# Batch norm with ReLU: loading the second half of x in one 8 MB transfer of 64 KB runs

## The chip, the cores and the metric

One core of a Trainium2 chip. The metric is the device time of one execution in microseconds (us), median of several runs. A profile's span is about 1.9 us shorter than the time of the same run (81.9 against 83.77 us). Timed comparisons are of runs at a granted clock of 1.0.

## The reference

```python
# x: (32, 128, 32, 32) float32; gamma, beta, running_mean, running_var: (128,)
normalized = (x - running_mean[None, :, None, None]) / np.sqrt(running_var[None, :, None, None] + eps)
scaled = normalized * gamma[None, :, None, None] + beta[None, :, None, None]
return np.maximum(scaled, 0).astype(np.float32)
```

16.78 MB come in, 16.78 MB go out, and each element needs one multiply, one add and one maximum.

## The kernel before

The 4096 rows (batch x channel) of 4 KB are laid out as 2 halves x 128 partitions x 16 rows, so that one partition of one half is a contiguous run of 64 KB. The whole input fits on the core at once, so every load can be issued at the start. Loads are issued from SyncE, stores from ScalarE. Both queues are served by the same 16 DMA engines: the packet times of loads and stores, divided by 16, add up to 96.2% of the span (prediction).

```python
J = 16
PIECES = (((0, 2), (2, 4), (4, 8), (8, 16)), ((0, 8), (8, 16)))
STORE_CUTS = {(0, 1)}
# ...
    tiles = []
    for t in range(T):
        for a, b in PIECES[t]:
            xt = data.tile([P, b - a, HW], F32, name=f"x{t}_{a}")
            nc.sync.dma_start(out=xt, in_=xr[t, :, a:b, :])
            tiles.append((t, a, b, xt))
# ... scale_t and bias_t are worked out from four small loads ...
    with tc.manual_schedule(engines={mybir.EngineType.Activation}):
        for t, a, b, xt in tiles:
            first = a
            for j in range(a, b):
                nc.scalar.activation(
                    out=xt[:, j - a, :], in_=xt[:, j - a, :], func=ACTF.Relu,
                    bias=bias_t[:, j : j + 1], scale=scale_t[:, j : j + 1],
                )
                if j + 1 == b or (t, j + 1) in STORE_CUTS:
                    nc.scalar.dma_start(
                        out=outr[t, :, first : j + 1, :], in_=xt[:, first - a : j + 1 - a, :]
                    )
                    first = j + 1
```

A piece of n rows is a transfer whose runs are n x 4 KB. One run of one partition is one packet on a DMA engine: the packet records of this kernel have 384 load packets of 32 KB for its three loads of 4 MB. That is 128 packets per transfer, 8 on each of the 16 engines.

## Time and profile before

| | before |
|---|---|
| time, 3 runs | 83.78 us (83.75 to 83.79) |
| span of the profile | 81.9 us |
| start of the first packet of x to end of the last packet | 1.84 to 80.61 us |
| mean time of the packets of one DMA engine | 78.75 us |
| ScalarE busy | 38.5 us, 47% |

### The profile page before, as it was taken

To read this page: it belongs to the slowest core of one execution; us is meant where nothing else is said; L and a number is where in the kernel's file an instruction comes from. 1 tells how busy PE (TensorE), PEld (TensorE's weight loads), DVE (VectorE), ACT (ScalarE), POOL (GpSimd) and SP (SyncE) were. 2 spreads that over 40 slices of the span, in tenths; PEclk is the share of its full clock that TensorE was granted. 3 is DMA by queue.
4 is the path that set the end of the run, shared out by engine and by line. 5 is a ranking of instruction groups with operands and counts; after the bars stand their busy time and mean duration, and the time that the engine had idled before them with its cause. 6 is when DMAs were issued, how large, how long until landed. Compare 5 with 4: busy or idle time off the path is not lost.

```text
span 81.9 us, 119 instructions
## 1 busy us (share of the span) xinstructions
PE 0.7 (1%) x2; PEld 0.5 (1%) x2; DVE 0.8 (1%) x5; ACT 38.5 (47%) x34; POOL 0.8 (1%) x6
## 2 busy tenths in 40 slices
PE   0002000000000000000000000000000000000000
PEld 0002000000000000000000000000000000000000
DVE  0000300000000000000000000000000000000000
ACT  0600377799039999199994199993000000000000
POOL 3000000000000000000000000000000000000000
DMA  2899999989899999979789798996999899799690
GB/s 32 328 425 472 408 448 448 512 352 494 370 448 416 446 418 396 500 296 600 320 380 580 304 464 384 512 512 288 480 512 400 368 512 448 320 512 496 272 512 0
DMA packets 1936, 33.56 MB, mean 410 GB/s; under 512 B 272, under 2 KB 272, under 8 KB 528
## 3 DMA queue, kind: packets, MB, share of 16 engines
q1 hardware_dynamic: 864, 16.78, 48.4%
q10 hardware_dynamic: 1072, 16.78, 47.8%
HBM read 16.78 MB, written 16.78 MB: 410 GB/s over the span
## 4 chain that ended last, share of the span: by engine, by line
DMA 56%; ACT 11%; SPq 0%; issue 0%
DMA x<-in_x_dram 56%; ACT x L96 11%; SPq L52 0%
## 5 line engine op out<-in xcount | busy, mean ns | idle before, releaser
L96 ACT ACTIVATE x<-x,bias_t,scale_t 128x1024 f32<-128x1024 f32 x32 | 37.0, 1228 | 10.3 <-DMA x<-in_x_dram 7.9
L82 ACT ACT_TABLE_LOAD x1 | 1.3, 1283 | 2.6 <-issue 2.6
L82 ACT ACTIVATE std_t<-cols,eps_t 128x16 f32<-128x16 f32 x1 | 0.3, 273 | 4.5 <-PE cols L74 4.5
L74 PE MATMUL cols<-raw,rep 8*128 8x64 f32 x2 | 0.7, 428 | 7.7 <-DMA raw<-in_beta_dram 7.7
L74 PEld LDWEIGHTS cols<-raw,rep 8*128 8x128 f32 x2 | 0.5, 304 | 7.7 <-issue 7.7
L64 POOL TENSOR_SCALAR_AFFINE_SELECT rep<-rep 8x128 f32<-8x128 f32 x1 | 0.4, 392 | 0.1
L84 DVE RECIPROCAL rstd_t<-std_t 128x16 f32<-128x16 f32 x1 | 0.3, 254 | 7.8 <-ACT std_t L82 7.8
L63 POOL MEMSET rep<- 8x128 f32 x1 | 0.2, 195 | 0.3 <-POOLq L124 0.3
L86 DVE TENSOR_TENSOR scale_t<-cols,rstd_t 128x16 f32<-128x16 f32 x1 | 0.2, 175 | 0.1
L90 DVE TENSOR_TENSOR bias_t<-cols,ms_t 128x16 f32<-128x16 f32 x1 | 0.2, 175 | 0.0
L88 DVE TENSOR_TENSOR ms_t<-cols,scale_t 128x16 f32<-128x16 f32 x1 | 0.2, 175 | 0.0
L124 POOL MEMSET const-bfloat16-1.0<- 128x1 bf16 x1 | 0.1, 106 | 0.0
L124 POOL MEMSET const-uint8-127<- 128x1 uint8 x1 | 0.1, 106 | 0.0
L124 POOL MEMSET const-float32-0.0<- 128x1 f32 x1 | 0.1, 103 | 0.3 <-issue 0.3
L124 POOL MEMSET const-float32-1.0<- 128x1 f32 x1 | 0.1, 103 | 0.0
L61 DVE MEMSET eps_t<- 128x1 f32 x1 | 0.1, 59 | 0.9 <-PEq L124 0.9
## 6 DMA issues: line engine op xcount, KB each, us to landing
x<-in_x_dram SPq DMA_DIRECT2D x3, 4096.0 KB, 38.8
out_dram<-x ACTq DMA_DIRECT2D x3, 4096.0 KB, 27.9
x<-in_x_dram SPq DMA_DIRECT2D x2, 1024.0 KB, 5.7
x<-in_x_dram SPq DMA_DIRECT2D x1, 2048.0 KB, 11.2
out_dram<-x ACTq DMA_DIRECT2D x1, 2048.0 KB
out_dram<-x ACTq DMA_DIRECT2D x2, 512.0 KB, 18.8
out_dram<-x ACTq DMA_DIRECT2D x1, 1024.0 KB
raw<-in_running_var_dram ACTq DMA_DIRECT2D x1, 0.5 KB
```

What stands on the lines that cost most here:

```text
L61: nc.vector.memset(eps_t, float(eps))
L63: nc.gpsimd.memset(rep, 1.0)
L64: nc.gpsimd.affine_select(out=rep, in_=rep, compare_op=mybir.AluOpType.is_equal, fill=0.0, base=0, pattern=[[0, P // Q], [-1, Q]], channel ...
L74: nc.tensor.matmul(cols.rearrange("p k j -> p (k j)"), rep.rearrange("q r s -> q (r s)"), raw.rearrange("q k j -> q (k j)"), start=True, s ...
L82: nc.scalar.activation(out=std_t, in_=cols[:, 0, :], func=ACTF.Sqrt, bias=eps_t[:, 0:1], scale=1.0)
L84: nc.vector.reciprocal(out=rstd_t, in_=std_t)
L86: nc.vector.tensor_mul(out=scale_t, in0=cols[:, 1, :], in1=rstd_t)
L88: nc.vector.tensor_mul(out=ms_t, in0=cols[:, 2, :], in1=scale_t)
L90: nc.vector.tensor_sub(out=bias_t, in0=cols[:, 3, :], in1=ms_t)
L96: nc.scalar.activation(out=xt[:, j - a, :], in_=xt[:, j - a, :], func=ACTF.Relu, bias=bias_t[:, j : j + 1], scale=scale_t[:, j : j + 1],)
L124: nc = _bacc.Bacc("TRN2", target_bir_lowering=False, num_devices=1)
```

## The change

The intent: one load instruction and one wait fewer, longer runs, and 16 transfers in all. The semaphores of the transfers rotate through eight, and SyncE waits for them at the end in a fixed order; with 16 transfers the last store's semaphore is the last in it.

```diff
-PIECES = (((0, 2), (2, 4), (4, 8), (8, 16)), ((0, 8), (8, 16)))
+PIECES = (((0, 2), (2, 4), (4, 8), (8, 16)), ((0, 16),))
 
-STORE_CUTS = {(0, 1)}
+STORE_CUTS = {(0, 1), (1, 8)}
```

## The prediction

> **What bounds the kernel now.** I read the page from its second part on: first which row is full from one end to the other, then what the queues carried, and only then the chain.
>
> The slices, the queues and the memory traffic of the page:
>
> ```profile
> ACT  0600377799039999199994199993000000000000
> ...
> DMA  2899999989899999979789798996999899799690
> ...
> q1 hardware_dynamic: 864, 16.78, 48.4%
> q10 hardware_dynamic: 1072, 16.78, 47.8%
> HBM read 16.78 MB, written 16.78 MB: 410 GB/s over the span
> ```
>
> ScalarE (ACT) is busy 47% of the span and has nothing to do in the last 12 slices. The DMA row has no hole from the second slice to the last but one. q1 (loads) and q10 (stores) together took 48.4 + 47.8 = 96.2% of 81.9 us, that is 78.8 us of each of the 16 DMA engines. The packet records of the trace start at 1.84 us and end at 80.61 us, 78.77 us later: every engine has a packet in hand at all times. So the kernel is bound by the bytes that the DMA engines move, and not by any instruction.
>
> The stretches confirm it (columns: stretch, its length, busy time of five engines, clock, DMA share, GB/s):
>
> ```profile
> 14.00:24.00 10.00, 0.00 (x0) 0.00 (x0) 0.00 (x0) 6.26 (x7) 0.00 (x0) 1.00 0.99 419
> 24.00:35.00 11.00, 0.00 (x0) 0.00 (x0) 0.00 (x0) 9.21 (x9) 0.00 (x0) 1.00 1.00 429
> 62.00:80.00 18.00, 0.00 (x0) 0.00 (x0) 0.00 (x0) 0.00 (x0) 0.00 (x0) 1.00 1.01 437
> ```
>
> Loads and stores together (24 to 35) move 429 GB/s, stores alone (62 to 80) 437; the stretches place whole packets by their start, so a few GB/s either way are counting. Mixing costs next to nothing.
>
> The chain that ended last is a trap here:
>
> ```profile
> 7.99 38.77 DMA x<-in_x_dram
> ...
> 46.79 9.16 ACT x L96 x8
> ```
>
> It says that the last load took 38.77 us and that the last eight ACTIVATEs follow. But that load is issued at 7.99 us and stands in a queue behind what is left of 12.6 MB of other loads. It ends at 46.76 us, and after it 34 us of stores still run, which the chain doesn't show. What ScalarE waits for is in the timeline:
>
> ```profile
> 23.86 9.16 ACT L96 ACTIVATE x<-x,bias_t,scale_t 128x1024 f32<-128x1024 f32 x8 [3.32 <-DMA x<-in_x_dram]
> 33.05 0.34 ACTq L104 DMA_DIRECT2D out_dram<-x  x1
> 34.81 9.16 ACT L96 ACTIVATE x<-x,bias_t,scale_t 128x1024 f32<-128x1024 f32 x8 [1.79 <-DMA x<-in_x_dram]
> 44.00 0.34 ACTq L104 DMA_DIRECT2D out_dram<-x  x1
> 46.79 9.16 ACT L96 ACTIVATE x<-x,bias_t,scale_t 128x1024 f32<-128x1024 f32 x8 [2.82 <-DMA x<-in_x_dram]
> 55.97 0.34 ACTq L104 DMA_DIRECT2D out_dram<-x  x1
> ```
>
> ScalarE waits 7.9 us for loads, and none of it reaches the end: the last store is issued at 55.97 us, while its first packet runs at 70.60 us (packet records). It waits in line for 14.6 us.
>
> The packet records give the cost of one packet (one contiguous run of one partition) on an engine:
>
> ```
> run      queue       count   median ns
>  4 KB    store        256      159
>  8 KB    load, store  384      309
> 16 KB    load, store  256      611
> 32 KB    load, store  768     1213
> ```
>
> **What the Trainium skill says.** "DMA: Bandwidth & Descriptors", section "Queues, rings and completion order", says that each DMA engine goes round-robin between the queue rows at packet granularity. The trace agrees: from 16 to 34 us a 32 KB load packet alternates with a 4 KB store packet, and the records give 378 to 383 GB/s of loads beside 48 to 49 of stores, 8 to 1. Its section "Where 436 GB/s comes from" puts the ceiling at 435.2 GB/s; by the packet records stores alone reach 433 to 434 here. So 33.55 MB can't take under 77.1 us (an estimate with the page's figure), against the 78.77 us seen. Its section "Anatomy of one DMA" has a fixed cost of about 2 us per DMA, mostly the receipt of the last write. The trace shows less of it at the only place where it is exposed: the last packet ends at 80.61 us and the last semaphore increment is in at 80.96, 0.35 us later. The other sixteen receipts lie under other transfers.
>
> **The change part by part.** Removed: one load instruction of SyncE, and its wait for an earlier load's semaphore. Merged: two loads of 4 MB (128 runs of 32 KB each) into one of 8 MB (128 runs of 64 KB). The stores stay seven, of the same sizes, and the 32 ACTIVATEs are the same; the build's order shows no other move. The instruction words still hold one element per partition for the new load, so I take it as 8 packets of 64 KB on each engine.
>
> 1. Packets. From 4 to 8 KB the cost rises by 150 ns, from 8 to 16 by 302, from 16 to 32 by 602: it is bytes plus some 9 ns. A 64 KB packet is then estimated at 1213 + 2 x 602 = 2417 ns, against 2426 for two of 32 KB. Eight on each engine: 8 x 9 = 0.07 us less. One semaphore packet of 9 ns less per engine, 0.01 us. This lies on the path that sets the end, because the DMA engines are never idle.
>
> 2. Load order. The load before the merged one ends its packets at 23.3 us, as now. The merged load then alternates with the second 4 KB store: 8 x (2417 + 159) = 20.6 us, so its packets end at 43.9 us and it lands at about 44.3 (0.35 to 0.7 us later, as now). Now the last load's packets end at 46.08 and it lands at 46.76. Loads win 2.2 us from stores because their packets are twice as large; the sum of work is unchanged.
>
> 3. ScalarE. It loses the early start on the second half (34.81 us now) and idles from 33.4 to 44.3 us, about 10.9 us. Then eight ACTIVATEs (9.16 us): the first 4 MB done at 53.5 us, store issued; eight more and the issue gap of 0.4 us: last store issued at about 63.0 us, 7 us later than now.
>
> 4. Do the stores run dry? At 43.9 us each engine still has the 8, 16 and 32 KB stores of the first half: 8 x (309 + 611 + 1213) = 17.1 us, to 61.0 us. The next store was issued at 53.5, 7.5 us ahead. It runs 8 x 1213 = 9.7 us, to 70.7; the last was issued at 63.0, 7.7 us ahead. The longest start that the trace shows is 3.65 us from issue to first packet (10.99 to 14.64 us, the first store, behind loads). So the queue stays full, with some 4 us in hand, and the late ScalarE costs nothing. The last packet ends at about 80.4 to 80.5 us.
>
> 5. The end. SyncE waits for the semaphores in a fixed order of double waits. Now the last store's semaphore is in the third, and two double waits (81.02 and 81.08 us) follow before the drain at 81.15. With 16 transfers over 8 semaphores the last store gets the one in the fifth, the last double wait, so those before it are passed during the transfer. That saves about 2 x 0.06 = 0.12 us.
>
> Sum: 0.07 + 0.01 + 0.12 = 0.20 us. 83.78 - 0.20 = 83.58 us, say 83.6.
>
> **The rivals.** *The queue runs dry*: ScalarE gets 8 MB at once, late, and the last stores come too late. For that, the merged load would have to land over 6 us later than 44.3 us. For: the idle time of ScalarE rises from 7.9 to about 14 us (3.3 + 10.9), and the last store's margin falls from 14.6 to 7.7 us. Against: the margins in step 4. If it landed at 52 us, the next store would be issued at 61.2 us, 0.2 us after the queue ran dry, and would start about 1.0 us later (the first load takes that from issue at 0.81 to first packet at 1.84 us): some 1.2 us lost, 84.8 us.
>
> *Long runs move faster*: the intent could be bandwidth. At most the 78.77 us shrink to 77.1, 1.7 us or 2.0%, if every byte went at the skill's ceiling; the change touches a quarter of the bytes, and the table of packets leaves 9 ns per packet to win. At best 83.3.
>
> *Long runs are slower*: nothing in the trace has a packet of 64 KB, and the records show some excess that is not a function of size: the first 8 KB load packets took up to 1026 ns (0.44 us per engine in sum), and 32 KB load packets beside stores up to 1386 ns (0.19 us per engine). If 64 KB packets were 2% slower than estimated, 8 x 48 ns = 0.4 us come back, and the time is 84.0. For a loss of over 2% they would have to be about 10% slower.
>
> *The 64 KB are cut in two inside*: then step 1 and 2 vanish, only the end is shorter, 83.65.
>
> **Range and chances.** The three runs before differ by 0.04 us, so the range is about mechanism, not noise. It holds the sum of step 1 and 5, the loss of either, and an excess of 64 KB packets of a few ns per KB: 83.35 to 83.85. Faster by 2% would be under 82.1 us, below what the ceiling allows: 1%. Slower by 2% is over 85.5 us and needs a dry queue of 2 us or packets 10% slower: 2%. Within 2%: 97%.
>
> **What would show it.** In the changed profile the DMA row should have no hole up to the last slice; the ACTIVATEs of the second half should start once, near 44.3 us (step 2; if near 46.5, the packets are cut), with an idle time before them near 11 us (step 3); the last store's issue should be near 63 us, and stores alone should still run at 433 to 437 GB/s (step 4); after the last landing no further double wait should stand before the drain (step 5: from the last landing to the drain 0.06 us and not 0.18). The packet records should show 128 packets of 64 KB near 2417 ns (step 1). The prediction is wrong if a hole stands in the DMA row between 60 and 72 us, or if load packets beside stores take longer per byte than now.

## The result, and the profile after

| | before | after |
|---|---|---|
| time, 6 runs each | 83.82 us (83.75 to 83.89) | 84.35 us (84.28 to 84.48) |
| ratio, 95% interval | | 1.0064 (1.0051 to 1.0077) |
| span of the profile | 81.89 | 82.49 |
| last packet ends | 80.61 | 81.32 |
| mean time of the packets of one engine | 78.75 | 79.37 |
| last landing to SyncE's drain | 0.18 | 0.08 |

A ratio here is the mean time of one kernel's fast runs over that of the other's in the same rounds, so not quite the ratio of the medians quoted beside it.

The change is within 2%, as given at 97%, but it goes the other way: 0.5 us slower where 0.2 us faster was predicted, and the time is outside the range. The interval lies clear of 1.

The page after, slices and queues, to set against those in the prediction:

```profile
ACT  0600477798049999000000999979999000000000
...
DMA  3899997969699965999956999997998999899690
...
q1 hardware_dynamic: 720, 16.78, 48.8%
q10 hardware_dynamic: 1072, 16.78, 47.4%
```

ScalarE has the hole that was expected (slices 17 to 22), and the stores have not run dry: after it the DMA row is as full as it was. The 5s and 6s up to slice 22 are no idle time. A slice counts a packet where it starts, and with 64 KB packets of 2.4 us, which are longer than a slice of 2.06 us, slices come out uneven. q1 has 144 packets less, but its share times the span has grown from 39.6 to 40.3 us per engine: fewer load packets took more time.

The timeline after, from the merged load's landing:

```profile
33.08 0.34 ACTq L104 DMA_DIRECT2D out_dram<-x  x1
45.19 9.16 ACT L96 ACTIVATE x<-x,bias_t,scale_t 128x1024 f32<-128x1024 f32 x8 [12.14 <-DMA x<-in_x_dram]
54.38 0.34 ACTq L104 DMA_DIRECT2D out_dram<-x  x1
54.77 9.16 ACT L96 ACTIVATE x<-x,bias_t,scale_t 128x1024 f32<-128x1024 f32 x8 [0.42 <-ACT x L96]
63.95 0.34 ACTq L104 DMA_DIRECT2D out_dram<-x  x1
```

The load landed at 45.17 and not at 44.3 us. The last store was issued at 63.95, and its first packet runs at 71.02 us (packet records): 7.1 us in line, so ScalarE's lateness costs nothing.

The stretches after, beside stores and with stores alone (columns as in the prediction):

```profile
24.00:34.00 10.00, 0.00 (x0) 0.00 (x0) 0.00 (x0) 9.05 (x8) 0.00 (x0) 1.00 1.02 439
...
62.00:80.00 18.00, 0.00 (x0) 0.00 (x0) 0.00 (x0) 1.92 (x2) 0.00 (x0) 1.00 1.01 435
```

No steady stretch is slower than before by more than the few GB/s of the counting (stores alone: 435 against 437). So the place to look is a passage between stretches, and the packet records of the trace show it. This is one DMA engine before the change and one after it, at the end of the loads. S is a store packet and L a load packet with its KB, each with its start in us and, where it took longer than the usual time of its size, by how many ns. (The kept records carry no engine number; packets are joined to an engine where one starts as another ends.)

```
before  38.38:S8 38.68:L32 39.89:S8 40.20:L32 41.41:S8 41.71:L32 42.92:S8 43.23:L32 44.44:S8 44.74:L32 45.95:S8 ...
after   35.76:S4 35.92:L64 38.33:S4 38.49:L64 40.90:S4 41.06:L64+646 44.12:S4 ...
```

After the change, seven of the eight 64 KB packets take 2418 ns. The eighth, the last packet of the load stream, takes 420 to 801 ns more, on every one of the 16 engines; the mean excess is 0.66 us. From here on, "loss" is this: the duration of a packet over the usual one of its size (159, 309, 460, 611, 1213, 2418 ns for 4, 8, 12, 16, 32, 64 KB), summed and divided by 16 engines.

The balance at the last packet, after minus before: start -0.02, eight packets of 2418 for sixteen of 1213 ns -0.06, one semaphore packet -0.01, loss at the start (8 KB packets) +0.06, loss in later load packets +0.64 (0.83 against 0.19), unevenness of the engines +0.10; sum +0.71 us. Then -0.01 to the last landing and -0.10 at SyncE's waits: +0.59 in the span with unrounded terms, which is the difference measured. "Unevenness", here and below, is what is left of the time from the first packet of x to the end of the last packet when the mean packet time of an engine is taken off (0.02 us before, 0.12 after): engines start and end at different times.

### The profile page after: what moved, and what is told of

Read it like the earlier page. It is cut to its first block, busy times and chain, and to the rows that moved or that the text cites. A ratio compares the mean times of both kernels' runs of the same rounds, so it can differ in the third digit from the quotient of the medians.

```text
span 82.5 us, 118 instructions
## 1 busy us (share of the span) xinstructions
PE 0.7 (1%) x2; PEld 0.5 (1%) x2; DVE 0.8 (1%) x5; ACT 38.5 (47%) x34; POOL 0.8 (1%) x6
## 4 chain that ended last, share of the span: by engine, by line
DMA 53%; ACT 21%; ACTq 1%; issue 1%
DMA x<-in_x_dram 46%; ACT x L96 21%; DMA raw<-in_running_mean_dram 6%; ACTq L59 1%; ACTq L104 0%
```

## The experiments

The question is what makes the last load packets long: the 64 KB runs, their place in the stream, what stands beside or behind them, or the moment. Each run gave the right output. "Before" under each run is the kernel before on the same chip in the same rounds. By the 2% rule every timed run but e9 has the verdict "same"; what is compared are smaller differences, with their intervals, and losses in the packet records.

**e1_no_first_cut: 16 transfers without 64 KB runs.**

```diff
# against the kernel before
-STORE_CUTS = {(0, 1)}
+STORE_CUTS = set()
```

> The kernel before with its first store uncut: 16 transfers, all loads in runs of 32 KB or less. It tells the end of the kernel from the 64 KB runs. If the semaphore order is worth what I claimed: 0.12 us at the end (last landing to drain near 0.06 us instead of 0.18) and 8 x 9 ns = 0.07 us for eight packets fewer, so 0.1 to 0.2 us faster than the kernel before. If the loss of the changed kernel came from having 16 transfers and not from the runs, this one would be about 0.5 us slower instead.

84.19 us (before 83.90), ratio 1.0038 (1.0018 to 1.0059). A miss: slower, not faster. The end did what was claimed (0.08 us from landing to drain), but the load packets lost 0.65 us instead of 0.19: 0.43 us of it at 12 to 24 us, where now 8 KB stores and not 4 KB ones set in beside the loads, and most of the rest at 38 to 44 us, where the 16 KB ones do. None of it was in the last load packets (0.01 us). So a loss of this kind needs no 64 KB packet, and it moves with the stores.

**e2_big_load_earlier: the 8 MB load ahead of the first half's last 4 MB.**

```diff
# against the changed kernel: loads and ScalarE both follow this order
+ORDER = ((0, 0, 2), (0, 2, 4), (0, 4, 8), (1, 0, 16), (0, 8, 16))
```

> The changed kernel with the 8 MB load issued ahead of the 4 MB load of the first half, so that other load packets stand behind it. In the changed kernel the eighth (last) 64 KB packet took 3.07 us instead of 2.418 on all 16 engines. Theory A (the last 64 KB packet of a transfer is long by itself): again about 0.65 us more on the last 64 KB packet, time like the changed kernel. Theory B (it is long because no load stands behind it in the load queue): all eight 64 KB packets at 2418 ns, and the time 0.5 to 0.7 us less than the changed kernel, near 83.7. Theory C (something at 41 to 44 us of the run, whatever is moved then): packets of that moment are long, about 0.6 us per engine, whichever they are.

84.60 us, ratio 1.0079 (1.0056 to 1.0102). The eight 64 KB packets lost 0.29 us in all, the last of them 0.18; the last two 32 KB packets of the stream, beside 4 KB stores, lost 0.82. Theory A falls: what was long in the changed kernel is not the last 64 KB packet as such. B holds for the place, but not with the time it foresaw: the loss went to the packets that are now last. C is not excluded by this run (41 to 45 us again).

**e3_beside_8k: 64 KB loads beside 8 KB stores.**

```diff
# against the changed kernel
-STORE_CUTS = {(0, 1), (1, 8)}
+STORE_CUTS = {(1, 8)}
```

> The changed kernel with the first store uncut, so that the 64 KB load packets run beside store packets of 8 KB and not of 4 KB, 15 transfers. If small stores beside the load make the last packet long (theory D), the excess of 0.65 us should shrink or go; if it is the load alone (A or B) it stays at 0.6 to 0.7 us and the time is the changed kernel's less 0.07, plus 0.06 for one double wait more at the end: 84.3.

84.47 us, ratio 1.0062 (1.0039 to 1.0086). The last 64 KB packet lost 0.23 us, a third of before; the stores beside it do count (D). The time didn't fall with it, because 0.40 us were lost earlier, where the 8 KB stores set in (as in e1), and the unevenness of the engines was 0.43 us.

**e4_one_queue: all stores in the loads' queue.**

```diff
# against the changed kernel
-                    nc.scalar.dma_start(
+                    nc.sync.dma_start(
```

> The changed kernel with all stores issued from SyncE, in the same queue as the loads, so that no store packet runs between load packets: the loads end near 40 us and the stores follow. If stores between the loads are needed for the long last packet (D), all 64 KB packets take 2418 ns and the time is about 83.5 to 83.7. A: the last one is long again, time near 84.3. B can't be told from D here, because store packets stand behind the load in the same queue. If SyncE gets to the stores too late, a hole in the DMA row near 40 us would show it.

84.75 us, ratio 1.0097 (1.0069 to 1.0125). No store runs between loads, and the loss is the greatest of all: nothing (0.00 us) from 5 us on, and then 1.34 us in the last 64 KB packet. D, that small stores between the loads cause it, falls; with them the loss was smaller (0.66 and 0.86 us in the changed kernel). One engine of this run:

```
33.95:L64 36.37:L64 38.78:L64+1298 42.49:(semaphore) 42.50:S4 42.66:S4 ...
```

**e5_one_queue_32k: the same with 32 KB runs.** The edit is that of e4, made to the kernel before.

> The kernel before (loads of 32 KB runs) with all stores issued from SyncE behind the loads, the partner of the one-queue run with 64 KB runs, which lost 1.34 us per engine in its last round of load packets and ended at 84.75. Theory R (the length of the run): no such loss, about 83.6 to 83.8. Theory S (the more the loads are let ahead of the stores, the more time the load packets lose, whatever their size): about as slow as the one-queue run with 64 KB, 84.5 to 84.9, the loss in the last load packets again.

84.81 us (before 83.89), ratio 1.0103 (1.0068 to 1.0137), loss 1.06 us in the last two 32 KB packets. That is as slow as e4. With the order of the transfers made the same, runs of 64 and of 32 KB end at the same time (84.75 and 84.81 us), and the losses (1.34 and 1.06) are about as far apart as two profiles of one kernel (0.2, r_after_again below): R falls as the main cause; S is not refuted. The page of e5:

```profile
DMA  2899896997999699899969999997999899899970
GB/s 44 315 418 485 378 599 284 504 504 331 426 504 489 268 504 504 347 410 504 252 246 432 465 441 418 520 457 331 473 489 410 378 489 457 363 441 489 441 331 0
```

The dip stands in slices 20 and 21 (252 and 246 GB/s, 39.5 to 43.7 us), where the loads end and the stores begin. (Single low slices such as 268 or 284 come from counting packets at their start; part of this dip does too.)

**e7_4k_beside_32k: 32 KB loads beside 4 KB stores up to their end.**

```diff
# against the kernel before
-STORE_CUTS = {(0, 1)}
+STORE_CUTS = {(0, 1), (0, 3)}
```

> The kernel before with the third store cut in two, so that store packets of 4 KB stand beside the 32 KB load packets up to the last load; loads take 8 of 9 parts of the traffic to their end, and not 4 of 5 as in the kernel before. R: the kernel before plus 0.07 for eight packets more, 83.9. S: 0.4 to 0.8 us slower than the kernel before, with the excess in the last load packets.

84.54 us, ratio 1.0076 (1.0034 to 1.0118), as S foresaw. The last two 32 KB packets lost 0.54 us; in the kernel before, where 8 KB stores stand beside them, 0.00. This is the changed kernel's loss, made in the kernel before without any 64 KB run, by eight small packets per engine more. (The run has one transfer more than the kernel before, too: from the last landing to the drain it took 0.25 us against 0.18.)

**e8_more_loads: another load behind the merged one.**

```diff
# against e4, behind the loads of x; nothing reads the tile
+    extra = data.tile([P, 8, HW], F32, name="extra")
+    nc.sync.dma_start(out=extra, in_=xr[0, :, 0:8, :])
```

> The one-queue kernel with 64 KB runs and one more load of 4 MB behind the merged load, into a tile that nothing reads (the output stays right). About 9.7 us longer. If the last load packets of the whole stream lose the time (end of the loads), the eight 64 KB packets are at 2418 ns and the loss moves to the last 32 KB packets near 50 us. If it is the last 64 KB packet of a transfer, or a moment near 39 to 42 us of the run, it stays where it was. If loads alone lose time again and again, the loss grows with the bytes.

94.41 us, one look. The eight 64 KB packets lost 0.02 us, and the last two packets of the stream, now 32 KB packets at 48 to 52.6 us, lost 1.26 us. One engine of this run (the stores, S, are in the same queue; semaphore packets are left out):

```
36.36:L64 38.77:L64 41.19:L32 42.40:L32 43.61:L32 44.82:L32 46.03:L32 47.24:L32 48.45:L32+646 50.31:L32+707 52.23:S4 ...
```

So it is neither the moment (C falls) nor the merged transfer nor the sum of bytes loaded, but the end of the stream of loads, wherever that is.

**r_after_again: the changed kernel's profile once more.**

> The changed kernel once more, for its profile: if the excess of 0.67 us per engine sits again in the eighth 64 KB packet of all 16 engines, it belongs to the kernel; if it sits elsewhere or differs much in size, it is a matter of the execution, and single profiles can't place it.

84.43 us, one look. The last 64 KB packet lost 0.86 us, on all 16 engines but with a spread up to 1.0 us. The place belongs to the kernel; the size is good to some 0.2 us.

**e11_hole_behind: nothing behind the loads.** ScalarE takes the second half first, so that no store can be issued before the last load has landed.

```diff
# against the changed kernel
-        for t, a, b, xt in tiles:
+        for t, a, b, xt in tiles[-1:] + tiles[:-1]:
```

> The changed kernel with the second half computed and stored first: no store can be issued before the last load has landed, and a hole of some 10 us stands between loads and stores (time about 93 us, output right). If the last load packets lose time by themselves at the end of a stream of loads, the 64 KB packets at the end have an excess of about 1 us per engine again. If they lose it to the stores that come behind (theory T), all 64 KB packets are at 2418 ns; a loss may then stand at the first stores instead.

95.25 us, one look. Its page, slices and rates:

```profile
DMA  2999999999999999900000999978999999799990
GB/s 60 371 425 469 427 490 448 448 448 448 448 448 448 448 448 448 448 0 0 0 0 0 448 448 448 434 322 364 448 448 378 413 441 448 336 448 448 448 448 0
```

The timeline of the same run, from the last load's landing to the first store:

```profile
42.05 9.16 ACT L96 ACTIVATE x<-x,bias_t,scale_t 128x1024 f32<-128x1024 f32 x8 [33.36 <-DMA x<-in_x_dram]
51.24 0.38 ACTq L104 DMA_DIRECT2D out_dram<-x  x1
```

448 GB/s slice after slice to the last load, then a hole. All 128 packets of 64 KB took 2418 ns, the longest too, and all load packets after the first 5.2 us together lost 0.01 us per engine. So the loads don't lose time by ending; they lose it when stores come behind them (T). Together with e8, where loads come behind loads and nothing is lost: the loss belongs to the passage from loads to stores. The first stores did not take it over, which the expectation had left possible: the store packets of this run lost 0.38 us per engine in all, but spread thinly over all of them (at most 0.01 in every other run).

**e9_16k_beside_64k: 16 KB stores beside 64 KB loads.**

```diff
# against the changed kernel
-PIECES = (((0, 2), (2, 4), (4, 8), (8, 16)), ((0, 16),))
+PIECES = (((0, 1), (1, 5), (5, 8), (8, 16)), ((0, 16),))
-STORE_CUTS = {(0, 1), (1, 8)}
+STORE_CUTS = {(1, 8)}
```

> The changed kernel with the first half cut at 1, 5 and 8 rows, so that store packets of 16 KB stand beside the 64 KB load packets to their end: loads 4 of 5 parts of the traffic at the end, the share of the kernel before, with the runs of the changed kernel; 15 transfers. R (the run's length costs): the excess of 0.6 to 0.8 us in the last 64 KB packets stays, time 84.2 to 84.4. S (the share of the loads at their end costs): the last 64 KB packets are at 2418 ns within 0.1 us, and the time is at or under the kernel before, 83.5 to 83.8.

85.78 us, ratio 1.0241. It is confounded by its own start: the first load in 4 KB runs, the small parameter loads landing 0.9 us later (8.46 us), and an unevenness of the engines of 1.04 us. The last 64 KB packets lost nothing, as S has it, but the same packets had lost 0.64 us from 28 us on, where the 16 KB stores set in. It can't be read as a time.

**e12_16k_second: the same mix with the start untouched.**

```diff
# against the changed kernel: ScalarE's order as (tile, first row, end), one store each
+        jobs = ((0, 0, 1), (2, 4, 8), (0, 1, 2), (1, 2, 4), (3, 8, 16), (4, 0, 8), (4, 8, 16))
```

> The changed kernel, same loads and same seven stores, only in another order: after the first 4 KB store comes the 16 KB one, then the second 4 KB and the 8 KB one. So the 64 KB load packets run beside 16 KB store packets (4 to 1, as in the kernel before) and not 4 KB ones (16 to 1), with the start untouched, which the run with other cuts had spoilt. If what counts is the share that stores have when the load stream ends: excess of the last 64 KB packet under 0.1 us (0.67 in the changed kernel), time 83.7 to 84.1; the loss that is left would stand where the 16 KB packets set in. If 64 KB packets lose it whatever is beside them: 0.6 us in the last packet, time 84.3.

84.21 us (before 83.84), ratio 1.0033 (1.0003 to 1.0062), just over the expected range. The last 64 KB packet lost 0.28 us instead of 0.66 to 0.86, the earlier 64 KB packets 0.2. So about half of the change's loss is got back by nothing but moving one store ahead of two others; under 0.1 was expected, so the share of stores isn't all.

**e10_same_mix_16: 16 transfers with the mix of before.**

```diff
# against the kernel before
-PIECES = (((0, 2), (2, 4), (4, 8), (8, 16)), ((0, 8), (8, 16)))
+PIECES = (((0, 4), (4, 8), (8, 16)), ((0, 8), (8, 16)))
-STORE_CUTS = {(0, 1)}
+STORE_CUTS = {(0, 1), (0, 2)}
```

> The kernel before with its first two loads merged into one (16 KB runs): the same stores beside the same 32 KB loads, but 16 transfers, so that the last store's semaphore is in the last double wait. From the end 0.10 us, from eight packets fewer 0.06 us: 0.1 to 0.2 us faster than the kernel before (ratio 0.998), last landing to drain 0.08 us. If the count of transfers does harm by itself, it is slower.

84.01 us (before 83.84), ratio 1.0022 (1.0008 to 1.0036). A miss. From landing to drain it took 0.08 us as claimed, but the later load packets lost 0.56 us and not 0.19, a little in each step, and the unevenness of the engines was 0.27 us against 0.02. The merged first load also let the first ACTIVATE start at 10.65 instead of 9.72 us, so the mix was not quite the same; whether that is why the losses rose isn't shown. The gain at the end is real (0.10 us) and smaller than the 0.37 us that the load packets lost more.

**r_before_again: the kernel before's profile once more.**

> The kernel before once more, for its profile: if the load packets of its last 4 MB again have next to no excess (0.04 us per engine, 0.19 over all 32 KB load packets), the difference to the changed kernel's 0.8 is the kernels'; if it has 0.5 or more, the placing in single profiles is loose.

83.84 us, one look. Loss in later load packets 0.23 us, 0.02 of it in the last two. In both profiles the kernel before is free of the loss in its last load packets.

All runs by what stands beside the last 64 KB of loads on each engine (packet records; loss per engine in us):

| run | load : store packet at the end | loss in the last 64 KB of loads | loss in load packets from 5.2 us to there |
|---|---|---|---|
| e4 | 64 KB alone, stores behind | 1.34 | 0.00 |
| e8 | 32 KB alone, stores behind | 1.26 | 0.03 |
| e5 | 32 KB alone, stores behind | 1.06 | 0.01 |
| after, twice | 64 : 4 | 0.66, 0.86 | 0.17, 0.23 |
| e2 | 32 : 4 | 0.82 | 0.34 |
| e7 | 32 : 4 | 0.54 | 0.31 |
| e3 | 64 : 8 | 0.23 | 0.40 |
| e12 | 64 : 16 | 0.28 | 0.28 |
| e10 | 32 : 8 | 0.12 | 0.44 |
| before, twice | 32 : 8 | 0.00, 0.02 | 0.19, 0.22 |
| e9 | 64 : 16 | 0.00 | 0.89 (spoilt start) |
| e1 | 32 : 16 | 0.01 | 0.64 |
| e11 | 64 KB alone, nothing behind | 0.00 | 0.01 |

From top to bottom the part that stores have when the loads end grows, on the whole, and the last load packets lose less. The order isn't strict: at 8 : 1, e2 and e7 (4 KB stores) lost 0.82 and 0.54 us, and e3 (8 KB stores) 0.23. The size of the store packet sorts the runs at least as well: 1.06 to 1.34 us with none beside, 0.54 to 0.86 with 4 KB, 0.00 to 0.23 with 8 KB, 0.00 to 0.28 with 16 KB. Share and store size change together in most of these runs, so which of them counts is not shown. Whether the load runs have 32 or 64 KB has no consistent sign.

Where stores come in earlier or with larger packets, part of the loss stands there instead (last column). The two columns together are what a kernel pays: 1.07 to 1.34 us with stores behind and none beside, 0.83 to 1.16 beside 4 KB stores, 0.56 to 0.89 in the other runs with larger stores, and only 0.19 and 0.23 in the kernel before.

## Why the prediction was wrong

**What bounds the kernel:** right. The times follow the packets of the DMA engines and not ScalarE, except in e11, which was built with a hole.

**Step 1, packets:** the usual cost was right to 1 ns (2418 against 2417), and the saving of 0.07 us for eight packets and a semaphore is in the balance (0.08 in the prediction's sum). What the step took for granted is that a packet costs what its size says. It doesn't at the last one: 3.08 us in the mean, the term of 0.66 us that the sum lacked. The rival "long runs are slower" had allowed 0.4 us, for the wrong reason: the seven others were not slow at all, and e5 and e7 lose it with 32 KB runs.

**Step 2, load order:** this is the step that failed. "Loads win 2.2 us from stores because their packets are twice as large; the sum of work is unchanged." The first half happened: the load packets ended at 44.64 us against 46.08 (43.9 foreseen; the difference is mostly the loss). The second half is false: the load packets after the first 5.2 us lost 0.83 us per engine where they had lost 0.19. To let the loads go ahead of the stores means to pass from loads to stores at the end in one step from 16 : 1, and that passage cost 0.66 us; in the kernel before the stores were let in at 8 : 1, then at 4 : 1, and 0.00 us were lost at the end. Merging the runs halved the turns of the stores, so that 4 KB stores, and not 8 KB ones, stood beside the last load. That this does the harm and not the length of the runs is shown by e7, which has the loss with 32 KB runs, and by e5; e12 gets only half of it back. The prediction's "Mixing costs next to nothing" was read from steady stretches and says nothing of the passages between them. The hint was in its own hands: it saw the 0.19 us of excess "beside stores" as not a function of size and gave it no cause, where in e1, e3 and e9 such excess stands at the places at which stores set in. And its own sign of being wrong, load packets beside stores that take longer per byte than now, came true.

**Steps 3 and 4, ScalarE and the dry queue:** right. ScalarE idled 12.1 us (10.9 foreseen; 0.9 of the difference is the later landing, the rest that the forecast counted from after the issue of the store, 33.4 and not 33.05 us), and the last store stood in line for 7.1 us (7.7 foreseen).

**Step 5, the end:** right, 0.10 us of 0.12, also in e1 and e10. Set against it, the later load packets lost 0.64 us more.

**Range:** 83.35 to 83.85 left 0.27 us for what packets of an unseen size might do. No trace at hand showed one, and the loss of 0.44 us in the first packets of the run showed that packets can take longer than their size says. The bounds of 2% were sound; the range was too narrow.

**The fixed cost:** the section "Anatomy of one DMA" that the prediction cites describes DMAs issued from GpSimd. Here they are issued from SyncE and ScalarE, so the 0.35 us seen is no test of its figure. Nothing in the sum rests on it.

**What stays open.** Shown is when the loss comes: stores behind the loads are needed (e11), and it is smaller when larger stores, or stores with a larger part, stand beside the last loads (table). Not shown is which of the two counts, nor why there is a loss. The records give each packet's duration and not where in the engine it waits. In e4, where no store runs between the loads, the records show the loads late before any store packet starts: the last of the 16 late load packets was due at 41.54 us, and the first store packet on any engine starts at 42.39. So whether the last reads are held up by the stores' first writes to HBM, or by work done for the stores before these records begin, can't be told. Nor is it settled why e12 still lost 0.28 us at 4 : 1 where the kernel before lost none, why e10, nearly the kernel before, lost 0.56 us in all against 0.19, or why the engines are uneven by up to 0.43 us in some of these kernels (1.04 in e9). No version tried beats the kernel before.

## What to carry to other kernels

When the DMA engines are always busy, how transfers are cut is also how loads and stores take turns, because turns go by packet: doubling the run of one side halves the turns of the other. Bring stores in while loads still run: here a jump from loads alone to stores alone cost 1.1 to 1.3 us at the end of the load stream, and 8 or 16 KB stores beside the last loads cut that to 0.0 to 0.3. That is no recipe yet: e1 and e10 had such stores too and lost 0.64 and 0.44 us earlier, where the stores set in, so look at the sum over all load packets. And when a sum of unchanged work is to predict a time, look in the packet records for where packets already take longer than their size says, and ask whether the change makes more of such places.

## What the Trainium skill lacked or had wrong

- "DMA: Bandwidth & Descriptors" has fixed and per-byte costs, but no cost for passing from loads to stores. Here it was 1.06 to 1.34 us per engine in the last load packets where stores followed loads at once, and 0.00 where nothing followed.
- The same page, section "Rules for kernel authors", says that spreading DMAs over several issuing engines doesn't help bandwidth and only saves issue time. For the rate of a steady stream this agrees with the runs (a 32 KB packet has the same 1213 ns with one queue and with two). But issuing stores from ScalarE, with loads on SyncE, lets them take turns and so spares most of the loss at the passage: 83.89 us, against 84.81 us with the same transfers all on SyncE (ratio 1.0103). The measurement decides: two queues were 1% better here.
- "SBUF — State Buffer", section "The DMA setup-cost knee", advises for DMA-bound transfers to coalesce into the largest single transfer, because of a fixed cost per transfer. The merged 8 MB load saved 8 ns per packet pair (2418 against 2 x 1213), and the kernel was 0.6% slower with it (84.35 against 83.82 us): beyond 4 MB the advice gained nothing that outweighed the worse passage to the stores.
